# One-core hybrid trunk: a thirteenth weight buffer for a fourth split pair, group norm by chunks, and the last small expert block behind the last wide one

## The chip, the core and the metric

The kernel runs on one core of one Trainium2 chip. The metric is the device time of one execution in microseconds; lower is better. Times of the kernel before come from three runs and from one more execution, which was profiled.

## What is computed

Two residual layers over 256 tokens of width 1024, in fp32. From the reference, cut:

```python
# each layer: x = x + W_out[concat(RWKV-7 | MLA | gMLP)(rms_norm(x) @ W_in)]
#             x = x + FFN(rms_norm(x))   dense SwiGLU in layer 0, top 2 of 8 SwiGLU experts in layer 1
# RWKV-7 part (6 heads of 64), after the scan over the tokens:
mu = jnp.mean(y, axis=-1, keepdims=True)
var = jnp.mean(jnp.square(y - mu), axis=-1, keepdims=True)
y = (y - mu) * lax.rsqrt(var + RWKV_GN_EPS)
y = y * ln_g + ln_b
y = y + jnp.sum(rh * kh * r_k, axis=-1, keepdims=True) * vh
y = y.reshape(B_, S_, A_WIDTH) * g
```

An expert has an inner width of 3584: 42 MiB of weights for gate, up and down projections, so the eight experts are 336 MiB, read from HBM once per execution.

## The kernel before

The program is `mix(0)`, `ffn()`, `mix(1)`, `experts()`.

**Arithmetic.** Products of full precision are made from two halves of a number: `split` (L192 to L198) makes a high part `wh` of 1024 columns on ACT (L196) and the rest `wl` on DVE (L197), and `mm3` (L200 to L203) issues three matmuls. A pair `wh`, `wl` comes from the pools `h_p` and `l_p`, three of each, and the experts have one pair more of their own (`NHL = 1`, pools `hi2` and `lo2`, L1173 to L1175; `own` in `units`, L1401).

**mix.** A layer's mix runs its parts as generators in the order of a string, `ORDER` (L38, L39): `R` is one step of the RWKV part, `o` one of `wout` (L403 to L429), `M` and `G` the other two parts. The RWKV scan works in four chunks of 64 tokens (the loop that begins behind `norm`): each chunk's products go through `R1` (a copy on DVE), `SA` and the state `M` to `ysb`. `norm(t)` (L743 to L765) then takes 128 tokens, two chunks, at a time: square on ACT (L748), reduction on DVE (L750), a power on POOL (L214 and L209, inside a helper), four products on DVE (L755), three transposes on TensorE (L759), two operations (L762, L763) and a copy and a subtract into `yTh` and `yTl` (L764, L765). `wout` has eight weight halves; three of them, n = 5, 6 and 7, need the result of `norm`, and for these it does the first 128 tokens for all three and then the second 128. At the end `x` gets the sums (L449 to L452).

**experts.** After the router the 336 loads of 1 MiB are issued by SP in one fixed order by `eload` (L1108 to L1117), into twelve buffers in a ring, `raw2` (8) and `raw` (4). Load 12 is the first that waits for a buffer. L1114 issues loads of an expert known beforehand and those of L1116 take the expert's number from a register that is read from `order` (L1180). The experts are sorted into places p = 0 to 7 by how many tokens they may take: wide blocks (128 tokens, p = 1, 2, 3, seven blocks each, 21 in all) use split weights; small blocks (64 tokens for p = 4, 5, 6, 32 for p = 0 and 7, 35 in all) use the weights as they come. A block is six loads, four for gate and up and two for down, and a load is two halves. In the trace, L1480 and L1496 are small blocks' gate and up, L1483 or L1498 their SiLU, L1507 to L1523 their transposes and transposed copies, L1550 their down products; L201 to L203 with `xg` are a wide block's gate and up, with `aT` its down products.

`work` and `halves` follow the same table, `TURNS` (L125): the number of small blocks after each wide one, the first two of the 35 (`LEAD`) coming before all wide ones. `fill` (L1427 on) issues splits ahead of `take`, with `AHEAD = 2` and `WINDOW = 10`. An expert's sums are scaled and added to `x` by `finish` (L1362 to L1387): a scaled copy and a subtract (L1371, L1372), matmuls (L1382, L1383) and adds (L1384); for the last expert each piece is stored as soon as it is added (L1692), eight stores.

Of the kernel before, what the change touches and what calls it, by code (L numbers as in the profile page):

```python
# [32 lines left out]
NHL = 1  # L33
# [4 lines left out]
ORDER = ("a5 R2 b c a2 R a3 M2 R X R2 y R2 M G R M G M o2 R o5",  # L38
         "a5 R2 b c a2 R a3 M2 R2 X R y R2 M G R M G M o2 R o5")  # L39
# [85 lines left out]
TURNS = [2] * 7 + [2, 1, 1, 2, 1, 2, 1] + [1, 1, 2, 1, 1, 2, 1]  # L125
# [4 lines left out]
def trunk(ctx: ExitStack, tc: tile.TileContext, x_in, pos_in, wst, moe, pp_in, rr_in, sw_in, rt_in,  # L130
# [60 lines left out]

    def split(t, a, b, hp=h_p, lp=l_p, E=None):  # L192
        n = b - a
        h = hp.tile([128, 1024], F32R, name="wh", tag="wh")
        lo = lp.tile([128, 1024], F32R, name="wl", tag="wl")
        act(h[:, 0:n], t[:, a:b], AF.Copy)  # L196
        (E or V).tensor_tensor(lo[:, 0:n], t[:, a:b], h[:, 0:n].bitcast(F32), op=ALU.subtract)  # L197
        return h, lo  # L198
# [95 lines left out]
    def mix(l):  # L294
        with ExitStack() as mctx:
# [107 lines left out]
            def wout():  # L403
# [21 lines left out]
                ws = [weights(n) for n in range(5, 8)]  # L425
                for t in range(2):
                    for n in range(5, 8):
                        part(n, t, *ws[n - 5])
                    yield  # L429
# [19 lines left out]
        for t in range(2):  # L449
            for nh in range(2):  # L450
                s_ = slice(nh * 512, nh * 512 + 512)
                V.tensor_tensor(x[:, t, s_], x[:, t, s_], acc[2 * t + nh], op=ALU.add)  # L452
# [6 lines left out]
    def rwkv(l, buf, wbuf, W, lz, z3, sg, pc, env):  # L459
# [283 lines left out]
        def norm(t):  # L743

            yTh, yTl = env["yh"], env["yl"]
            yt = ysb[:, t * 6:t * 6 + 6, :]
            sq = buf("shp", (128, 514))[:, 0:384].rearrange("p (u v) -> p u v", u=6)
            act(sq, yt, AF.Square)  # L748
            ss = small([128, 6], name="gn_ss")
            V.tensor_reduce(ss, sq, axis=AX.X, op=ALU.add)  # L750
            r = rsqrt(pre_eps(ss, 6, 1.0 / 64, GN_EPS, "gn"), 6, "gn")
            yn = buf("shp", (128, 514))[:, 0:384].rearrange("p (i h v) -> p i h v", i=3, h=2)
            for cp in range(2):
                for hv in range(2):
                    V.tensor_tensor(yn[HALF[cp], :, hv, :], yt[HALF[hv], cp * 3:cp * 3 + 3],  # L755
                                    r[HALF[hv], cp * 3:cp * 3 + 3, None].to_broadcast([64, 3, 64]), op=ALU.mult)
            ps = pb()
            for i in range(3):
                T.transpose(ps[:, i * 128:i * 128 + 128], yn[:, i].rearrange("p h v -> p (h v)"), ident)  # L759
            ts = slice(t * 128, t * 128 + 128)  # L760
            ya = ga[:, :, ts]
            V.tensor_tensor(ya, ps[:, 0:384].rearrange("p (i s) -> p i s", i=3), ya, op=ALU.mult)  # L762
            V.tensor_tensor(ya, ya, bv[:, :, ts], op=ALU.add)  # L763
            act(yTh[:, 0:3, ts], ya, AF.Copy)  # L764
            V.tensor_tensor(yTl[:, 0:3, ts], ya, yTh[:, 0:3, ts].bitcast(F32), op=ALU.subtract)  # L765

        M = None
        for c in range(4):
# [24 lines left out]
            act(ysb[:, c * 3:c * 3 + 3, :], ps, AF.Copy)  # L793
            if c == 1:
                yield
                norm(0)
                yield
        yield
        norm(1)
# [300 lines left out]
    def experts():  # L1100
# [7 lines left out]
        def eload(e, j):  # L1108
            i = cnt_loads[0]
            cnt_loads[0] += 1  # L1110
            pool = raw2_p if i % (4 + NRAW2) < NRAW2 else raw_p
# [60 lines left out]
        ap_ = ctx.enter_context(tc.tile_pool(name="moa", bufs=2, reuse_waits="tile"))  # L1172
        if NHL:  # L1173
# [119 lines left out]
        assert len(TURNS) == len(wides) and LEAD + sum(TURNS) == len(narrows)  # L1293
# [114 lines left out]
        def halves():  # L1408
# [4 lines left out]
            for n in range(len(wides) + 1):  # L1413
                if n < len(wides):
                    yield from units(*wides[n], range(4))
                if n > 0:
# [3 lines left out]
                before = narrows[m:m + TURNS[n]] if n < len(wides) else []  # L1420
# [145 lines left out]
        def work():  # L1566
# [8 lines left out]
            for n in range(len(wides) + 1):  # L1575
# [26 lines left out]
                new = narrows[m:m + TURNS[n]] if n < len(wides) else []  # L1602
# [244 lines left out]
```

## Time and profile before

| | us |
|---|---|
| median of 3 runs | 1409.38 |
| lowest, highest | 1407.07, 1413.32 |
| the profiled execution | 1410.85 |
| its span | 1409.0 |
| TensorE busy | 1330.4 (94%) |
| DVE busy | 714.6 (51%) |
| ACT busy | 628.3 (45%) |
| packets of SP's loads, share of 16 DMA engines over the span | 73.3% |

The span is the time from the first to the last instruction of the profiled execution; 1.85 us lie around it. The profiled execution is 1.47 us above the median. TensorE's mean granted clock is 0.968 of 2.4 GHz. A busy share is an average over stages: the experts' stage begins near 560 us.

### The profile page before, as it was taken

What the parts mean: (1) busy time and instruction counts of PE and PEld (TensorE: products, weight loads), DVE (VectorE), ACT (ScalarE), POOL (GpSimd) and SP (SyncE); (2) the same over time, 40 slices, a digit from 0 to 9 for tenths busy, and PEclk for the clock granted to TensorE, in tenths of its full rate; (3) what the DMA queues carried; (4) which work ended last, traced back from release to release, by engine and by line L of the source; (5) the groups of instructions that cost most, each with busy time, mean ns of one, the idle gap of its engine ahead of it and who ended that gap; (6) DMA issues with size and microseconds to landing.
All of it is one profiled execution on the core that took longest, in us unless ns stands there. A gap on an engine that the chain in (4) does not pass through costs nothing. (4 is left out here: it accounts for less than half of the span.)

```text
span 1409.0 us, 24079 instructions
## 1 busy us (share of the span) xinstructions
PE 1330.4 (94%) x9860; PEld 966.7 (69%) x9860; DVE 714.6 (51%) x1053; ACT 628.3 (45%) x986; POOL 77.3 (5%) x126
## 2 busy tenths in 40 slices
PE   7988899999999888999999999999999999999986
PEld 7977678888888777775666555755766656667653
DVE  5685455455576655453335314535544446556443
ACT  7558254444475652453324313423434345444442
POOL 2250000000115110000000000000000000000000
PEclk9999999999999998999999999999999999999997
DMA  7410244555452251899999999999999999999995
GB/s 285 179 61 2 90 149 180 181 188 188 147 195 103 65 222 60 341 384 426 425 426 425 426 395 368 427 381 426 407 426 414 416 426 427 426 420 426 426 426 213
DMA packets 60437, 422.63 MB, mean 300 GB/s; under 512 B 7200, under 2 KB 8224, under 8 KB 10400
## 3 DMA queue, kind: packets, MB, share of 16 engines
q1 hardware_dynamic: 59760, 420.03, 73.3%
q8 instruction: 79, 1.29, 0.4%
q10 hardware_dynamic: 560, 1.00, 0.2%
q14 instruction: 38, 0.31, 0.1%
HBM read 419.95 MB, written 1.05 MB: 299 GB/s over the span
## 5 line engine op out<-in xcount | busy, mean ns | idle before, releaser
L197 DVE TENSOR_TENSOR wl<-raw,wh 128x1024 fp32r<-128x1024 f32 (+1 forms) x370 | 439.4, 1219 | 176.3 <-ACT wh L196 173.2
L196 ACT ACTIVATE wh<-raw 128x1024 fp32r<-128x1024 f32 (+1 forms) x370 | 379.9, 1053 | 224.1 <-PE pb L203 113.2
L202 PE MATMUL pb<-wl,xg 128*128 128x512 f32 x336 | 141.0, 420 | 12.6 <-DVE wl L197 12.0
L1480 PE MATMUL pb<-raw,xgs 128*64 128x256 f32 x1344 | 151.0, 380 | 0.0
L201 PE MATMUL pb<-wh,xg 128*128 128x512 f32 x336 | 135.5, 406 | 7.8 <-ACT wh L196 7.8
L203 PE MATMUL pb<-wh,xg 128*128 128x512 f32 x336 | 133.6, 398 | 0.0
L1480 PEld LDWEIGHTS pb<-raw,xgs 128*64 128x64 f32 x1344 | 95.0, 137 | 54.7 <-issue 9.1
L1550 PE MATMUL pa<-raw,aT 128*32 128x256 f32 (+1 forms) x1008 | 120.7, 454 | 0.6 <-ACT aT L1523 0.6
L1496 PE MATMUL pb<-raw,xgs 128*32 128x256 f32 x1344 | 93.0, 402 | 9.5 <-DMA raw<-moe 9.4
L202 PEld LDWEIGHTS pb<-wl,xg 128*128 128x128 f32 x336 | 63.9, 190 | 40.4 <-DVE wl L197 23.1
L1483 ACT ACTIVATE a<-pb,rg 128x256 f32<-128x256 f32 x21 | 10.0, 474 | 178.2 <-PE pb L1480 178.2
L1511 DVE TENSOR_TENSOR aT<-pb,aT 128x512 fp32r<-128x512 f32 x21 | 14.5, 692 | 144.9 <-ACT aT L1510 144.8
L1550 PEld LDWEIGHTS pa<-raw,aT 128*32 128x32 f32 (+1 forms) x1008 | 42.3, 118 | 63.6 <-issue 49.0
L201 PEld LDWEIGHTS pb<-wh,xg 128*128 128x128 f32 x336 | 63.8, 190 | 29.6 <-ACT wh L196 15.3
L1496 PEld LDWEIGHTS pb<-raw,xgs 128*32 128x32 f32 x1344 | 46.1, 115 | 50.2 <-issue 14.0
L202 PE MATMUL pb<-wl,hTh 128*128 128x512 f32 (+1 forms) x192 | 73.0, 380 | 0.0
L203 PEld LDWEIGHTS pb<-wh,xg 128*128 128x128 f32 x336 | 64.2, 191 | 11.8
L203 PE MATMUL pb<-wh,hTl 128*128 128x512 f32 (+1 forms) x192 | 71.6, 376 | 0.0
L202 PE MATMUL pa<-wl,aT 128*128 128x512 f32 x168 | 69.2, 412 | 0.2 <-DVE wl L197 0.2
L201 PE MATMUL pb<-wh,hTh 128*128 128x512 f32 (+1 forms) x192 | 67.4, 377 | 0.7 <-ACT hTh L284 0.7
L203 PE MATMUL pa<-wh,aT 128*128 128x512 f32 x168 | 66.3, 394 | 0.0
L1485 DVE SCALAR_TENSOR_TENSOR a<-pb,rg,a 128x256 f32<-128x256 f32 x21 | 10.2, 484 | 99.4 <-PE pb L1480 99.4
(383 smaller groups left out, 2060.4 us busy)
## 6 DMA issues: line engine op xcount, KB each, us to landing
raw<-moe SPq DMA_DIRECT2D x336, 1024.0 KB, 11.9
raw<-wst SPq DMA_DIRECT2D x54, 1024.0 KB, 4.8
raw<-wst SPq DMA_DIRECT2D x4, 832.0 KB, 5.0
area<-sw_in SPq DMA_DIRECT2D x2, 960.0 KB, 6.7
area<-sw_in SPq DMA_DIRECT2D x2, 664.0 KB, 6.2
x<-x_in SPq DMA_DIRECT2D x2, 512.0 KB, 5.3
raw<-wst SPq DMA_DIRECT2D x2, 512.0 KB, 7.1
out_dram<-x SPq DMA_DIRECT2D x8, 128.0 KB, 2.3
```

The source lines that it names most:

```text
L196: act(h[:, 0:n], t[:, a:b], AF.Copy)
L197: (E or V).tensor_tensor(lo[:, 0:n], t[:, a:b], h[:, 0:n].bitcast(F32), op=ALU.subtract)
L201: T.matmul(o, lhsT=xh, rhs=wh, start=first, stop=False)
L202: T.matmul(o, lhsT=xh, rhs=wl, start=False, stop=False)
L203: T.matmul(o, lhsT=xl, rhs=wh, start=False, stop=last)
L1480: T.matmul(ps[HALF[hv], :], lhsT=z[:, k, :], rhs=w[:, o_:o_ + 256], start=(k == 0), stop=(k == KD - 1))
L1483: act(a, ps, AF.Silu, scale=rs[0])
L1485: V.scalar_tensor_tensor(a, ps, rs[0], a, op0=ALU.mult, op1=ALU.mult)
L1496: T.matmul(ps[QUART[g], :], lhsT=z[:, k, :], rhs=ws[g // 2 * 4 + k // 2][:, o_:o_ + 256], start=(k == 0), stop=(k == KD - 1))
L1511: V.tensor_tensor(z[:, :, 1, :], p3, z[:, :, 0, :].bitcast(F32), op=ALU.subtract)
L1550: T.matmul(acc[rows, :], lhsT=aT[:, f, :], rhs=ws[f][:, g * w:g * w + w], start=(i == 0 and f == 0), stop=(i == NB - 1 and f == 3))
```

## The change

- `NHL` is 0: the experts have three split pairs, not four. In place of the fourth pair a pool `raw3` holds a thirteenth weight buffer, and the ring of `eload` is 13 long.
- The last seven entries of `TURNS` become eight: the last small block (place 7, block 6) comes after the last wide block's down products, for which `work` and `halves` go round once more; `drain()` (which finishes the additions to `x` that are under way) comes ahead of it.
- `norm` takes one chunk: a reduction over 3 columns instead of 6, two products instead of four. A new `finish(t)` does transposes, the two operations, copy and subtract in three pieces of 128 columns.
- In `ORDER` the last steps are `o6 R o2`, not `o2 R o5`, and `wout` has one more `yield`. `norm` of the last chunk is issued behind the last split's subtract, and the additions to `x` behind the last subtract of `finish(1)`.

```diff
-NHL = 1
+NHL = 0
-ORDER = ("a5 R2 b c a2 R a3 M2 R X R2 y R2 M G R M G M o2 R o5",
-         "a5 R2 b c a2 R a3 M2 R2 X R y R2 M G R M G M o2 R o5")
+ORDER = ("a5 R2 b c a2 R a3 M2 R X R2 y R2 M G R M G M o6 R o2",
+         "a5 R2 b c a2 R a3 M2 R2 X R y R2 M G R M G M o6 R o2")
-TURNS = [2] * 7 + [2, 1, 1, 2, 1, 2, 1] + [1, 1, 2, 1, 1, 2, 1]
+TURNS = [2] * 7 + [2, 1, 1, 2, 1, 2, 1] + [1, 1, 2, 1, 1, 2, 0, 1]
...
-        (E or V).tensor_tensor(lo[:, 0:n], t[:, a:b], h[:, 0:n].bitcast(F32), op=ALU.subtract)
+        last_split[0] = (E or V).tensor_tensor(lo[:, 0:n], t[:, a:b], h[:, 0:n].bitcast(F32), op=ALU.subtract)
...
                 ws = [weights(n) for n in range(5, 8)]
+                yield
...
-        for t in range(2):
-            for nh in range(2):
-                s_ = slice(nh * 512, nh * 512 + 512)
-                V.tensor_tensor(x[:, t, s_], x[:, t, s_], acc[2 * t + nh], op=ALU.add)
+        with tc.issue_after(env["end"].ins):
+            for t in range(2):
+                for nh in range(2):
+                    s_ = slice(nh * 512, nh * 512 + 512)
+                    V.tensor_tensor(x[:, t, s_], x[:, t, s_], acc[2 * t + nh], op=ALU.add)
...
-        def norm(t):
+        yn = [buf("shp", (128, 514))[:, 0:384].rearrange("p (i h v) -> p i h v", i=3, h=2) for _ in range(2)]
+
+        def norm(c):
+
+            t, cp = divmod(c, 2)
+            yt = ysb[:, c * 3:c * 3 + 3, :]
+            sq = vf.tile([128, 3, 64], F32, name="sq", tag="R1", bufs=2)
+            act(sq, yt, AF.Square)
+            ss = small([128, 3], name="gn_ss")
+            V.tensor_reduce(ss, sq, axis=AX.X, op=ALU.add)
+            r = rsqrt(pre_eps(ss, 3, 1.0 / 64, GN_EPS, "gn"), 3, "gn")
+            for hv in range(2):
+                V.tensor_tensor(yn[t][HALF[cp], :, hv, :], yt[HALF[hv]],
+                                r[HALF[hv], :, None].to_broadcast([64, 3, 64]), op=ALU.mult)
+
+        def finish(t):
...
             for i in range(3):
+                T.transpose(ps[:, i * 128:i * 128 + 128], yn[t][:, i].rearrange("p h v -> p (h v)"), ident)
+                ya = ga[:, i, ts]
+                V.tensor_tensor(ya, ps[:, i * 128:i * 128 + 128], ya, op=ALU.mult)
+                V.tensor_tensor(ya, ya, bv[:, i, ts], op=ALU.add)
+                act(yTh[:, i, ts], ya, AF.Copy)
+                last = V.tensor_tensor(yTl[:, i, ts], ya, yTh[:, i, ts].bitcast(F32), op=ALU.subtract)
+            return last
...
             act(ysb[:, c * 3:c * 3 + 3, :], ps, AF.Copy)
+            if c % 2 == 0:
+                norm(c)
             if c == 1:
                 yield
-                norm(0)
+                norm(1)
+                finish(0)
                 yield
         yield
-        norm(1)
+        with tc.issue_after(last_split[0].ins):
+            norm(3)
+        env["end"] = finish(1)
...
-            pool = raw2_p if i % (4 + NRAW2) < NRAW2 else raw_p
+            j_ = i % (5 + NRAW2)
+            pool = raw2_p if j_ < NRAW2 else raw_p if j_ < NRAW2 + 4 else raw3_p
...
+        raw3_p = ctx.enter_context(tc.tile_pool(name="raw3", bufs=1, reuse_waits="tile"))
...
-            for n in range(len(wides) + 1):
+            for n in range(len(TURNS) + 1):
...
                 small_downs(before, nT)
-                new = narrows[m:m + TURNS[n]] if n < len(wides) else []
+                if n == len(wides):
+                    drain()
+                new = narrows[m:m + TURNS[n]] if n < len(TURNS) else []
```

A program sets the order of each engine's instructions from this code and from priorities, so the places that matter are shown as it came out. Line numbers of the changed kernel are two higher near `split` and some sixteen higher in the experts.

On SP, at the start of the experts' loads, before (L1116 are loads 12 and 13; they come behind seven reads of `order` at L1180, the last of which is shown, and one of a flag at L1612; ahead of the reads stand loads 0 to 11 of L1114):

```order
L1180 TENSOR_LOAD order
L1180 ISA x2
L1612 TENSOR_LOAD flag_i
L1612 ISA x2
L1116 ISA
L1116 DMA raw<-moe 128x2048
L1116 ISA
L1116 DMA raw<-moe 128x2048
```

and changed (L1129 are loads 0 to 11, L1131 load 12, L1196 the reads):

```order
L1129 DMA raw<-moe 128x2048 x12
L1196 TENSOR_LOAD order
L1196 ISA x2
L1131 ISA
L1131 DMA raw<-moe 128x2048
L1196 TENSOR_LOAD order
L1196 ISA x2
```

Load 12 moved from behind all the reads to right behind the first; load 13 is now the first behind them.

On ACT, from one wide block of the first expert that has them to the next, before (L196 splits, L1461 the wide block's SiLU, L1498 and L1523 the 32-token block that goes with it, L1483, L1510 and L1523 the small blocks of 64 tokens):

```order
L196 ACTIVATE wh<-raw 128x1024 x6
L1461 ACTIVATE a<-pb,rg 128x512
L196 ACTIVATE wh<-raw 128x1024 x6
L1498 ACTIVATE a<-pb,rg 64x256
L1523 ACTIVATE aT<-pb 128x2x2x64 x2
L1483 ACTIVATE a<-pb,rg 128x256 x2
L1510 ACTIVATE aT<-pb 128x4x128
L1523 ACTIVATE aT<-pb 128x2x2x32
L196 ACTIVATE wh<-raw 128x1024 x7
```

and changed (L198 splits, the others sixteen lines further down):

```order
L198 ACTIVATE wh<-raw 128x1024 x6
L1477 ACTIVATE a<-pb,rg 128x512
L198 ACTIVATE wh<-raw 128x1024 x5
L1514 ACTIVATE a<-pb,rg 64x256
L1539 ACTIVATE aT<-pb 128x2x2x64 x2
L198 ACTIVATE wh<-raw 128x1024
L1499 ACTIVATE a<-pb,rg 128x256 x2
L1526 ACTIVATE aT<-pb 128x4x128
L1539 ACTIVATE aT<-pb 128x2x2x32
```

One split, the first half of the next wide block, moved ahead of the small blocks' SiLU; on DVE its subtract moved with it.

On TensorE, at the end of the program, before (L201 to L203 are the last wide block's down products, L1550 the last small block's, L1382 and L1383 what `finish` multiplies):

```order
L201 MATMUL pa<-wh,aT 128x512 x2
L1550 MATMUL pa<-raw,aT 32x256 x8
L202 MATMUL pa<-wl,aT 128x512
L203 MATMUL pa<-wh,aT 128x512
L202 MATMUL pa<-wl,aT 128x512
L203 MATMUL pa<-wh,aT 128x512
L1550 MATMUL pa<-raw,aT 32x256 x8
L1382 MATMUL pb<-oh,pT 128x512 x4
L1383 MATMUL pb<-ol,pT 128x512 x4
L1382 MATMUL pb<-oh,pT 128x256 x2
L1383 MATMUL pb<-ol,pT 128x256 x2
```

and changed (L203 to L205, L1566, L1398 and L1399 in their place; L1512 and L1536 are the last small block's gate and up and its transposes):

```order
L203 MATMUL pa<-wh,aT 128x512 x2
L204 MATMUL pa<-wl,aT 128x512
L205 MATMUL pa<-wh,aT 128x512
L204 MATMUL pa<-wl,aT 128x512
L205 MATMUL pa<-wh,aT 128x512
L1398 MATMUL pb<-oh,pT 128x512 x4
L1399 MATMUL pb<-ol,pT 128x512 x4
L1512 MATMUL pb<-raw,xgs 32x256 x32
L1536 MATMUL pb<-cc,a 128x64 x2
L1566 MATMUL pa<-raw,aT 32x256 x16
L1398 MATMUL pb<-oh,pT 128x256 x4
L1399 MATMUL pb<-ol,pT 128x256 x4
```

The last small block moved behind the last wide block and behind what `finish` does for it.

## Rows read from the trace of the kernel before

**Rows 1.** The page: busy time of the engines, and what the DMA moved in 40 slices.

```profile
PE 1330.4 (94%) x9860; PEld 966.7 (69%) x9860; DVE 714.6 (51%) x1053; ACT 628.3 (45%) x986; POOL 77.3 (5%) x126
...
GB/s 285 179 61 2 90 149 180 181 188 188 147 195 103 65 222 60 341 384 426 425 426 425 426 395 368 427 381 426 407 426 414 416 426 427 426 420 426 426 426 213
```

**Rows 2.** Windows: each engine's busy time (instructions), granted clock, DMA share, GB/s.

```profile
860.00:880.00 20.00, 20.00 (x139) 10.64 (x141) 3.84 (x5) 3.14 (x6) 0.00 (x0) 1.00 0.87 343
...
1340.00:1360.00 20.00, 14.22 (x99) 9.31 (x100) 10.52 (x10) 10.77 (x14) 0.00 (x0) 0.91 1.01 426
```

**Rows 3.** The chain of waits, its last step through the loads: start, duration, link.

```profile
1363.31 19.78 DMA raw<-moe
```

**Rows 4.** SP's own timeline at loads 11 and 12: start, duration, instruction.

```profile
538.50 0.33 SPq L1114 DMA_DIRECT2D raw<-moe  x1
568.78 2.63 SPq L1116 DMA_DIRECT2D raw<-moe  x4
```

**Rows 5.** The page, costliest groups: busy, mean ns of one, idle before and releaser.

```profile
L197 DVE TENSOR_TENSOR wl<-raw,wh 128x1024 fp32r<-128x1024 f32 (+1 forms) x370 | 439.4, 1219 | 176.3 <-ACT wh L196 173.2
L196 ACT ACTIVATE wh<-raw 128x1024 fp32r<-128x1024 f32 (+1 forms) x370 | 379.9, 1053 | 224.1 <-PE pb L203 113.2
L202 PE MATMUL pb<-wl,xg 128*128 128x512 f32 x336 | 141.0, 420 | 12.6 <-DVE wl L197 12.0
```

**Rows 6.** Timelines of ACT and then TensorE at one wide block's start.

```profile
790.81 0.47 ACT L1483 ACTIVATE a<-pb,rg 128x256 f32<-128x256 f32 x1 [6.43 <-PE pb L1480]
...
793.76 3.90 ACT L196 ACTIVATE wh<-raw 128x1024 fp32r<-128x1024 f32 x4
798.39 1.06 ACT L196 ACTIVATE wh<-raw 128x1024 fp32r<-128x1024 f32 x1 [0.73 <-PE pb L203]
799.79 1.06 ACT L196 ACTIVATE wh<-raw 128x1024 fp32r<-128x1024 f32 x1 [0.33 <-PE pb L203]
...
795.15 0.50 PE L201 MATMUL pb<-wh,xg 128*128 128x512 f32 x1
796.93 0.50 PE L202 MATMUL pb<-wl,xg 128*128 128x512 f32 x1 [1.29 <-DVE wl L197]
```

**Rows 7.** The weight buffers in 1360 to 1400 us, and the timeline of the end.

```profile
L1116 SPq DMA_DIRECT2D raw<-moe x5: 333/333/333, 1360.9 to 1371.0; - x5
...
DMA to landing us min/median/max: 19.4/19.8/19.8
...
1392.52 1.07 PE L1550 MATMUL pa<-raw,aT 128*32 128x256 f32 x16
...
1398.22 5.31 SPq L1692 DMA_DIRECT2D out_dram<-x  x8
```

**Rows 8.** Layer 0's mix at its end: timelines of DVE, POOL, TensorE; TensorE's windows.

```profile
165.05 1.23 DVE L197 TENSOR_TENSOR wl<-raw,wh 128x1024 fp32r<-128x1024 f32 x1 [1.57 <-ACT wh L196]
...
168.14 1.28 DVE L452 TENSOR_TENSOR x<-x,pa 128x512 f32<-128x512 f32 x2 [1.40 <-PE pa L203]
...
167.12 1.33 POOL L209 TENSOR_TENSOR rq_y<-pe,cc 128x6 f32<-128x6 f32 x1
...
168.18 0.40 PE L203 MATMUL pa<-wh,hTl 128*128 128x512 f32 x1
...
173.24 0.79 PE L201 MATMUL pa<-wh,hTh 128*128 128x512 f32 x1 [1.79 <-ACT hTh L764]
...
160.00:168.00 8.00, 8.00 (x43) 1.00 0.53 201
173.00:179.00 6.00, 5.76 (x14) 0.50 0.00 0
```

**Rows 9.** Layer 1's mix at its end: timeline of TensorE.

```profile
532.79 0.45 PE L739 MATMUL pb<-SA,TrbT 64*64 64x64 f32 x8
...
540.04 1.25 PE L1142 MATMUL pa<-cc,x 128*128 128x128 f32 x8
...
542.25 0.50 PE L201 MATMUL pa<-wh,hTh 128*128 128x512 f32 x1 [0.96 <-ACT hTh L764]
```

More of the change, by code (lines that the diff above doesn't have):

```diff
@@ L190, in load @@
         return t
+    last_split = [None]
     def split(t, a, b, hp=h_p, lp=l_p, E=None):
@@ L741, in chain_mm @@
             return ps[:, 0:192].rearrange("p (u c) -> p u c", u=3)
-        def norm(t):
-            yTh, yTl = env["yh"], env["yl"]
[L746 to L756, printed above, removed]
+        yn = [buf("shp", (128, 514))[:, 0:384].rearrange("p (i h v) -> p i h v", i=3, h=2) for _ in range(2)]
@@ L757, in norm @@
+        def finish(t):
+            yTh, yTl = env["yh"], env["yl"]
+            ts = slice(t * 128, t * 128 + 128)
             ps = pb()
             for i in range(3):
[L759 to L763, printed above, removed]
@@ L764, in norm @@
-            act(yTh[:, 0:3, ts], ya, AF.Copy)
-            V.tensor_tensor(yTl[:, 0:3, ts], ya, yTh[:, 0:3, ts].bitcast(F32), op=ALU.subtract)
+                T.transpose(ps[:, i * 128:i * 128 + 128], yn[t][:, i].rearrange("p h v -> p (h v)"), ident)
[4 more added lines that the diff above has]
+                last = V.tensor_tensor(yTl[:, i, ts], ya, yTh[:, i, ts].bitcast(F32), op=ALU.subtract)
@@ L1292, in experts @@
         narrows = [(p, i) for p in NARROWS for i in range(NB)]
-        assert len(TURNS) == len(wides) and LEAD + sum(TURNS) == len(narrows)
+        assert len(TURNS) == len(wides) + 1 and LEAD + sum(TURNS) == len(narrows)
         ask(0)
@@ L1412, in halves @@
                     yield from units(*b, js)
-            for n in range(len(wides) + 1):
+            for n in range(len(TURNS) + 1):
                 if n < len(wides):
                     yield from units(*wides[n], range(4))
-                if n > 0:
+                if 0 < n <= len(wides):
                     yield from units(*wides[n - 1], (4, 5))
@@ L1419, in halves @@
                     yield from units(*b, (4, 5))
-                before = narrows[m:m + TURNS[n]] if n < len(wides) else []
+                before = narrows[m:m + TURNS[n]] if n < len(TURNS) else []
                 m += len(before)
@@ L1574, in work @@
             ask(NARROWS[1])
-            for n in range(len(wides) + 1):
+            for n in range(len(TURNS) + 1):
                 if wjob is not None:
```

## The prediction

> **What bounds the kernel now.** I read the page first, then 20 us windows, then the chain of waits and the queue of SP, and last three short timelines. The page's 40 slices say that from about 600 us on 426 GB/s come in nearly without a break [rows 1]: 1 MiB in 2.46 us. Behind that are the experts' 336 loads, all issued by SP. The windows show where the stream falls short: 343 GB/s in 860 to 880 us, while TensorE is busy for 20.00 of 20 us; but in 1340 to 1360 us the DMA is full and TensorE is busy for 14.22 us only [rows 2]. So two bounds take turns: between about 740 and 1020 us the buffers are full and TensorE decides, later the stream does. The chain agrees: before its last 26 us it runs back through DMA alone, three steps of eight loads, the last one 19.78 us [rows 3], which is 2.47 us a load. A microsecond gained anywhere before the last landing thus counts only if it makes the loads start earlier; one gained behind the last landing counts whole.
>
> **The thirteenth buffer.** Loads 0 to 11 go into twelve free buffers. Load 12 is the first that must wait for one: it goes out at 568.78 us with the next three, 30 us after load 11 at 538.50 [rows 4]. With thirteen, every load waits for the buffer of one load earlier. That is worth one place in the stream, once: **-2.4 us** [rows 3], for the buffer is refilled at the same rate afterwards. Nothing delays it: in the new order of SP load 12 stands right behind the first read of the register `order`, which it needs. Bounds: 0 and -4.9 (two places).
>
> **Three split pairs.** A half of a wide load costs ACT 1.05 us and, behind it, DVE 1.22 us [rows 5]; TensorE needs 1.40 us for its six matmuls, the distance at which pairs come free in the block shown (ACT, waiting for L203, starts at 798.39 and 799.79) [rows 6]. A pair is thus held for 1.05 + 1.22 + about 0.2 of hand-over + 1.40 = 3.9 us. Shared among three that is 1.29 us a half, below TensorE's 1.40: three just keep up, while nothing else comes between on ACT and DVE. That the pairs are scarce is in the page: ACT waits 113.2 us in all for L203, the last reader of a pair [rows 5]. For a block I take 0.
>
> **The start of a wide block.** In the block shown ACT makes four splits in a row from 793.76, so all four pairs had been free; the first began only then because it stood in line behind the SiLU and the transposed copies of the small block. TensorE has its high half at 795.15 and its low half at 796.93, with 1.29 us of idle time [rows 6]. In the new order one split stands ahead of that SiLU, on ACT and on DVE. TensorE's idle time for low halves is 12.6 us over all 336 such matmuls [rows 5]; about a third of the expert stage (280 of 850 us) is bound by TensorE, so about **-4.0 us** reach the stream there. Ends: 0 (three pairs shorten the lead as much as the order lengthens it) and -9.0 (seven blocks between 745 and 1012 us at 1.29).
>
> **The end.** The last load lands 19.4 us after its issue, at 1371.0 + 19.4 = 1390.4 us; the first store goes out at 1398.22 [rows 7]: 7.8 us, in which TensorE still does a wide load's second half, L1550 only at 1392.52, both blocks' results and the adds to x. Now the last wide block, with its sums, lies ahead of the last loads, and behind the last landing are left at most the 16 matmuls of L1550 (1.07 us), one scaled copy and one subtract over 128x256 (0.47 us each, as the SiLU over as many [rows 6]), two matmuls and one add, with hand-over about 1.2 us. That is some 3.3 us. So **-4.5 us**. The eight stores behind stay (0.66 us apart, to the end of the span 10.8 us after the first); SP issues nothing else there. Ends: -3.0, if TensorE's clock, granted at 0.91 in 1340 to 1360 us where it waits for loads [rows 2], is low there, and -5.2.
>
> **The tail of mix, layer 0.** In the old order the last split ends at 166.28 us, the run of matmuls at 168.58, and they go on at 173.24 us only: between lie the group norm over six columns, with 1.33 us on POOL, and two adds to x (0.64 us each), which stand ahead of the norm's products on DVE [rows 8]. For chunk 3 alone, ready behind the split: reduction 0.35, POOL 0.20 + 0.85 (estimated for three columns, between half and all of the 1.33), two products 0.72, one transpose 0.33, two ops of 0.26, copy 0.30, and 0.5 of hand-over: 3.8 us, so 170.1. Against it stands that all of chunk 3's products now come ahead of the run, where before they were put between its matmuls; TensorE then waits for R and SA, and R waits on DVE for chunk 2's norm: +1.5. Sum **-1.6 us**, ends +1 and -5.0. The second end is the clock: behind the wait, in 173 to 179 us, it is granted at 0.50, that is 1.2 GHz, and 14 matmuls take 6 us, while in 160 to 168 us it is 1.00, 2.4 GHz, and 43 take 8 [rows 8]. Those 14 would take 2.6 us at the full clock's pace (14 x 8 / 43), 3.4 less; of this I count none, and all of it in the second end. By "TensorE: Matmul & The Clock Gate" of the Trainium skill, section "HAM oscillation — how this bites in real kernels", idle stretches between matmuls bring the lower clock; by that rule a shorter wait may keep the higher one, and this term would be -5.0.
>
> **The tail of mix, layer 1.** Old: chunk 3's last product at 533.24 us, matmuls of the second half of the tokens resumed at 542.25, with six matmuls of the last weight and waits for it in between [rows 9]. New: the product comes after 20 matmuls of the run (533.6 to 534.05, by the same run's pace); ysb, square and reduction 1.1, POOL and products 1.9, hand-over 0.4, so the transposes come near 537.4 and the first piece of hTh 1.3 later, at 538.7: -3.5. But the eight transposes of x for the router (1.25 us) filled that wait before [rows 9] and now follow the adds to x, behind the run: **-2.3 us**. Ends 0 and -4. The ffn between the layers moves as a whole, and so does the router.
>
> Sum: 2.4 + 4.0 + 4.5 + 1.6 + 2.3 = 14.8 us. The profiled execution took 1410.85 us (span 1409.0), so 1396.1; the median of the runs, 1409.38, is 1.5 below it, so **1394.6**, say 1395.
>
> **Rivals.**
> - *Three pairs starve TensorE (slower).* If adds to x (0.64 us) and SiLU (0.47 us) [rows 6, 8] fall between the splits, a pair is held for 5.0 us, 1.67 a half, 0.27 more than TensorE needs: 12 halves make 3.2 us a wide block. Seven blocks up to 1012 us make 23 us, all of it in the stream; from 0.18 us a half on, the change loses. With no gain at the block starts: 1394.6 + 4.0 + 23 = **1422**. For it speaks the 113.2 us, against it that ACT and DVE are busy for 45% and 51% of the span only [rows 1]. 0.08.
> - *The sure part alone.* The block starts stay, the mixes give nothing: 2.4 + 3.0 = 5.4, so **1404**, which is no change (within 0.5%, 7 us, about what a measurement here can tell). For it: the dips of rows 2 are TensorE's, and a buffer does not make it faster. 0.17.
> - *The early split holds the SiLU.* Where loads are late (from 1310 us on) the split placed ahead now waits for its load, and the small block's SiLU, its products and transposed copies, some 1.6 us, come after it instead of in the wait. The stream hides that except in the last such block: +1.6, and without the gain at block starts **1400**. The splits of rows 6 that stood behind the SiLU with pairs free show that ACT keeps its order. The Trainium skill's "TensorE: Matmul & The Clock Gate", section "Architectural detail: the array is 16× 32×32, not 1× 128×128", says the same of ACT and DVE, strict first-in, first-out. 0.10.
> - *More.* Layer 0 keeps its clock (-3.4 more) and the block starts give all (-5.0 more): **1386**. 0.15.
> - The forecast: 0.50.
>
> **How the numbers follow.** The forecast's own cases lie between 1389 and 1400. Eight in ten are held from just under the lower case, 1385, to the sure part alone, 1404; left out are the starved TensorE and a little at both ends. Faster by over 0.5% means below 1402.3: the forecast, the lower case and nearly all of the third rival, 0.74. Within: the sure part and the rest, 0.18. Slower: the starved TensorE, 0.08.
>
> **What would show it.** The first store about 3 us behind the last landing; load 12 issued by some 5 us sooner after load 11, and each later load at least one place earlier; no idle time of TensorE for L199 at the starts of wide blocks, and the low windows of 820 to 1020 us filled; matmuls resumed near 171.6 us in layer 0 and some 3 us earlier in layer 1. Wrong would be: TensorE waiting for L199 in the middle of wide blocks, or the same low windows with the stream shifted by 2.4 us only.

## The result, and the profile after

| | us |
|---|---|
| before, median of 11 runs (lowest, highest) | 1411.38 (1407.07, 1413.32) |
| changed, median of 11 runs (lowest, highest) | 1417.07 (1414.76, 1426.99) |
| ratio, 95% interval | 1.0053 [1.0036, 1.0070] |
| profiled execution of the changed kernel, span | 1414.76, 1412.9 |

The kernel became slower by half a per cent where 1395 was forecast. The thirteenth buffer and the new end did about what they were to do; the new norm did more than that in layer 0 and nothing in layer 1. The loss is in the blocks of the experts between about 690 and 1023 us, in which the profile shows no idle time of TensorE that had not been there before.

The page of the changed kernel, where it answers to [rows 1, 5] (L198 and L199 are the splits, L203 to L205 a wide block's three matmuls, L1566 the small blocks' down products):

```profile
PE 1345.2 (95%) x9860; PEld 966.5 (68%) x9860; DVE 724.3 (51%) x1081; ACT 635.4 (45%) x998; POOL 79.5 (6%) x134
...
L199 DVE TENSOR_TENSOR wl<-raw,wh 128x1024 fp32r<-128x1024 f32 (+1 forms) x370 | 444.7, 1220 | 197.2 <-ACT wh L198 192.3
L198 ACT ACTIVATE wh<-raw 128x1024 fp32r<-128x1024 f32 (+1 forms) x370 | 384.0, 1054 | 252.5 <-PE pb L205 157.3
L204 PE MATMUL pb<-wl,xg 128*128 128x512 f32 x336 | 142.3, 424 | 11.7 <-DVE wl L199 10.9
...
L1566 PE MATMUL pa<-raw,aT 128*32 128x256 f32 (+1 forms) x1008 | 131.8, 456 | 1.0 <-ACT aT L1539 1.0
```

ACT waits 157.3 us for the last reader of a pair (L205), before 113.2: the pairs are scarcer. But TensorE waits for them no longer than it did (10.9 us for low halves, before 12.0). It is busy for 14.8 us more, with the same 9860 instructions: the number to explain.

The windows, for [rows 2]:

```profile
820.00:840.00 20.00, 20.00 (x131) 10.08 (x127) 0.00 (x0) 0.47 (x1) 0.00 (x0) 1.00 0.83 306
860.00:880.00 20.00, 20.00 (x122) 9.91 (x121) 7.31 (x7) 5.36 (x7) 0.00 (x0) 1.00 0.76 307
```

At the full clock (1.00) TensorE is busy throughout, but in 860 to 880 us it gets through 122 matmuls where it got through 139, and the stream falls to 307 GB/s where it had 343. (The work in the two windows is not quite the same, for the blocks begin 4 to 5 us later by then; the table of block starts below counts the same work.)

SP's timeline at loads 11 and 12, for [rows 4], and at the stores:

```profile
527.71 0.33 SPq L1129 DMA_DIRECT2D raw<-moe  x1
553.26 0.35 SPq L1131 DMA_DIRECT2D raw<-moe  x1
...
1404.09 4.26 SPq L1710 DMA_DIRECT2D out_dram<-x  x8
```

The weight buffers behind 1371 us, for [rows 7]:

```profile
L1131 SPq DMA_DIRECT2D raw<-moe x5: 332/333/333, 1371.2 to 1381.0; - x5
...
DMA to landing us min/median/max: 19.5/19.5/19.9
```

Load 12 goes out 15.5 us earlier, the last load 10.0 us later. It lands 10.5 us later, at 1400.9 us. From there to the end of the span it is 12.0 us, before 18.6.

The start of every wide block (its first matmul on TensorE, from the two traces; blocks are counted from 0) says where that turns:

| wide block | 0 | 3 | 4 | 5 | 6 | 7 | 8 | 10 | 14 |
|---|---|---|---|---|---|---|---|---|---|
| before, us | 584.3 | 697.8 | 745.9 | 795.1 | 844.8 | 893.7 | 941.6 | 1013.5 | 1160.4 |
| changed, us | 579.2 | 692.8 | 743.9 | 795.8 | 848.4 | 899.2 | 949.1 | 1023.4 | 1172.8 |
| difference | -5.1 | -5.0 | -2.0 | +0.6 | +3.6 | +5.4 | +7.5 | +10.0 | +12.4 |

5.1 us are gained by the time the wide blocks begin, and 15.1 us are lost in blocks 3 to 9, which TensorE bounds: 315.6 us became 330.7. Block 5 shows how. A piece of it on TensorE before (L1496 are gate and up products of the 32-token block that runs beside the wide one; the trace has two records for each small matmul, so x30 are 15):

```profile
802.71 1.93 PE L1496 MATMUL pb<-raw,xgs 128*32 128x256 f32 x30
804.57 0.50 PE L202 MATMUL pb<-wl,xg 128*128 128x512 f32 x1
...
806.16 0.64 PE L1496 MATMUL pb<-raw,xgs 128*32 128x256 f32 x8
806.73 0.50 PE L202 MATMUL pb<-wl,xg 128*128 128x512 f32 x1
...
820.71 0.40 PE L203 MATMUL pa<-wh,aT 128*128 128x512 f32 x1
820.95 0.40 PE L202 MATMUL pa<-wl,aT 128*128 128x512 f32 x1
821.19 0.40 PE L203 MATMUL pa<-wh,aT 128*128 128x512 f32 x1
821.52 8.51 PE L1550 MATMUL pa<-raw,aT 128*32 128x256 f32 x54
```

and changed (L1512 are those products):

```profile
802.80 0.39 PE L205 MATMUL pb<-wh,xg 128*128 128x512 f32 x1
803.03 0.40 PE L203 MATMUL pb<-wh,xg 128*128 128x512 f32 x1
803.36 1.91 PE L1512 MATMUL pb<-raw,xgs 128*32 128x256 f32 x26
805.20 0.50 PE L204 MATMUL pb<-wl,xg 128*128 128x512 f32 x1
805.54 0.39 PE L205 MATMUL pb<-wh,xg 128*128 128x512 f32 x1
...
806.79 1.05 PE L1512 MATMUL pb<-raw,xgs 128*32 128x256 f32 x10
807.77 0.50 PE L204 MATMUL pb<-wl,xg 128*128 128x512 f32 x1
...
811.30 0.64 PE L1512 MATMUL pb<-raw,xgs 128*32 128x256 f32 x8
811.87 0.50 PE L203 MATMUL pb<-wh,xg 128*128 128x512 f32 x1
...
814.63 0.62 PE L1512 MATMUL pb<-raw,xgs 128*32 128x256 f32 x2
815.18 0.66 PE L1536 MATMUL pb<-cc,a 128*128 128x128 f32 x4
```

A matmul of the 32-token block (128*32 in the lines) fills 32 of 128 columns; four of them begin within 0.02 us of each other, so four are called a group here. A piece is a row of small matmuls between others, and a cut is a place where the wide ones are left for such a piece.

The price of a cut is in the starts. From one wide matmul to the next it is 0.23 us (802.80 to 803.03), from a wide to a small one 0.33 (to 803.36), and the first step among the wide ones after that is 0.34 (805.20 to 805.54). A piece of one small matmul takes 0.55 us until the next engine step (814.63 to 815.18), one of four 0.57 (811.30), one of five 0.98 (806.79), one of fifteen 1.86 (802.71, before): 0.41 to 0.43 for each group begun, however few of the four there are, and 0.14 on top. So a cut costs 0.10 + 0.11 + 0.14 = 0.35 us, and 0.41 more where it leaves a group unfilled; all of it counts as busy time. In the order of TensorE, which was there to be read ahead of the run, the 32 gate and up matmuls of this block stand in pieces of 15, 4, 5, 1 and 7 before, and of 13, 5, 4, 4, 5 and 1 now; the 16 down matmuls were 2, 3 and 11, and are 5, 3, 3, 1 and 4. Over the whole program 88 such pieces became 121, and 694 begun groups (of four, or of two for 64 tokens) 709.

In blocks 3 to 9 TensorE goes from wide to small matmuls 44 times, before 22, and begins 12 groups more: 22 x 0.35 + 12 x 0.41 = 12.6 of the 15.1 us lost there. (From wide matmuls to transposes and other matmuls of 128 columns it goes 35 times, before 34.)

### The profile page after: what moved, and what is told of

The parts are those of the page before. It is cut to its first block, busy times and chain, and to the rows that moved or that the text cites. A ratio compares the mean times of both kernels' runs of the same rounds, so it can differ in the third digit from the quotient of the medians.

```text
span 1412.9 us, 24147 instructions
## 1 busy us (share of the span) xinstructions
PE 1345.2 (95%) x9860; PEld 966.5 (68%) x9860; DVE 724.3 (51%) x1081; ACT 635.4 (45%) x998; POOL 79.5 (6%) x134
## 3 DMA queue, kind: packets, MB, share of 16 engines
q8 instruction: 79, 1.29, 0.4%
## 4 chain that ended last, share of the span: by engine, by line
PE 83%; DVE 6%; ACT 3%; DMA 3%; POOL 2%; issue 2%; SPq 0%; DVEq 0%; ACTq 0%; POOLq 0%
PE pb L1496 10%; PE pa L1566 9%; PE pb L204 9%; PE pb L205 8%; PE pb L203 8%; PE pa L204 6%; PE pa L203 6%; PE pb L1512 6%; PE pa L205 6%; DVE wl L199 3%; DMA raw<-moe 3%; PE pb L1268 1%; PE pa L373 1%; PE pa L374 1%; PE pa L375 1%
## 5 line engine op out<-in xcount | busy, mean ns | idle before, releaser
L199 DVE TENSOR_TENSOR wl<-raw,wh 128x1024 fp32r<-128x1024 f32 (+1 forms) x370 | 444.7, 1220 | 197.2 <-ACT wh L198 192.3
L198 ACT ACTIVATE wh<-raw 128x1024 fp32r<-128x1024 f32 (+1 forms) x370 | 384.0, 1054 | 252.5 <-PE pb L205 157.3
L204 PE MATMUL pb<-wl,xg 128*128 128x512 f32 x336 | 142.3, 424 | 11.7 <-DVE wl L199 10.9
L1496 PE MATMUL pb<-raw,xgs 128*64 128x256 f32 x1344 | 152.5, 381 | 0.0
L203 PE MATMUL pb<-wh,xg 128*128 128x512 f32 x336 | 136.9, 410 | 5.1 <-ACT wh L198 5.1
L205 PE MATMUL pb<-wh,xg 128*128 128x512 f32 x336 | 134.1, 399 | 0.0
L1496 PEld LDWEIGHTS pb<-raw,xgs 128*64 128x64 f32 x1344 | 97.4, 137 | 52.6 <-issue 8.2
L1566 PE MATMUL pa<-raw,aT 128*32 128x256 f32 (+1 forms) x1008 | 131.8, 456 | 1.0 <-ACT aT L1539 1.0
L1512 PE MATMUL pb<-raw,xgs 128*32 128x256 f32 x1344 | 94.6, 399 | 3.9 <-DMA raw<-moe 3.7
L1566 PEld LDWEIGHTS pa<-raw,aT 128*32 128x32 f32 (+1 forms) x1008 | 42.9, 118 | 67.7 <-issue 55.2
L1527 DVE TENSOR_TENSOR aT<-pb,aT 128x512 fp32r<-128x512 f32 x21 | 14.5, 692 | 140.9 <-ACT aT L1526 140.9
L203 PEld LDWEIGHTS pb<-wh,xg 128*128 128x128 f32 x336 | 64.1, 191 | 28.8 <-ACT wh L198 12.1
L1512 PEld LDWEIGHTS pb<-raw,xgs 128*32 128x32 f32 x1344 | 45.5, 114 | 45.1 <-issue 15.5
L205 PEld LDWEIGHTS pb<-wh,xg 128*128 128x128 f32 x336 | 64.5, 192 | 11.4
L205 PE MATMUL pb<-wh,hTl 128*128 128x512 f32 (+1 forms) x192 | 71.7, 377 | 0.2 <-DVE hTl L287 0.2
L203 PE MATMUL pb<-wh,hTh 128*128 128x512 f32 (+1 forms) x192 | 67.5, 378 | 0.1
L205 PE MATMUL pa<-wh,aT 128*128 128x512 f32 x168 | 66.5, 396 | 0.0
```

The costliest lines, as they stand in the source:

```text
L199: last_split[0] = (E or V).tensor_tensor(lo[:, 0:n], t[:, a:b], h[:, 0:n].bitcast(F32), op=ALU.subtract)
L203: T.matmul(o, lhsT=xh, rhs=wh, start=first, stop=False)
L204: T.matmul(o, lhsT=xh, rhs=wl, start=False, stop=False)
L205: T.matmul(o, lhsT=xl, rhs=wh, start=False, stop=last)
L1496: T.matmul(ps[HALF[hv], :], lhsT=z[:, k, :], rhs=w[:, o_:o_ + 256], start=(k == 0), stop=(k == KD - 1))
L1512: T.matmul(ps[QUART[g], :], lhsT=z[:, k, :], rhs=ws[g // 2 * 4 + k // 2][:, o_:o_ + 256], start=(k == 0), stop=(k == KD - 1))
```

## The experiments

Two theories stood against each other. *Cuts*: with three pairs the program that orders the instructions puts small matmuls between the wide halves more often (presumably because it expects a half later), and each cut costs TensorE time. *Starved*: three pairs make TensorE wait for halves (the prediction's rival at 1422), and the cuts are only its sign. Three more runs take the change's other parts alone. The table has the time with its ratio to the kernel before on the same chip, and for blocks 3 to 9 of the profiled execution their duration, the passages of TensorE from wide to small matmuls, and the groups begun beyond the least that these matmuls need (these from the order).

| kernel | us | ratio, 95% interval | blocks 3 to 9, us | passages | groups |
|---|---|---|---|---|---|
| before | 1410.7 to 1411.8 | | 315.6 | 22 | 7 |
| changed | 1417.07 | 1.0053 [1.0036, 1.0070] | 330.7 | 44 | 19 |
| e1 three pairs | 1430.60 | 1.0141 [1.0113, 1.0168] | 329.0 | 45 | 18 |
| e3 three pairs, 13 buffers | 1427.67 | 1.0122 [1.0098, 1.0146] | 331.0 | 47 | 20 |
| e2 the rest of the change | 1405.51 | 0.9960 [0.9943, 0.9977] | 316.5 | 19 | 8 |
| e7 norm alone | 1409.01 | 0.9986 [0.9961, 1.0011] | 316.4 | 19 | 8 |
| e8 last block alone | 1405.14 | 0.9960 [0.9936, 0.9984] | 315.7 | 22 | 7 |
| e4 changed, first join | 1410.48 | 0.9999 [0.9979, 1.0019] | 321.2 | 23 | 6 |
| e5 changed, both joins | 1396.34 | 0.9882 [0.9850, 0.9914] | 311.4 | 11 | 0 |
| e6 four pairs, both joins | 1399.63 | 0.9908 [0.9879, 0.9937] | 310.7 | 9 | 0 |
| e9 before, first join | 1407.90 | 0.9974 [0.9951, 0.9996] | 308.9 | 10 | 0 |
| e10 four pairs, cut on purpose | 1417.48 | 1.0045 [1.0022, 1.0068] | 327.4 | 50 | 5 |

By the prices above, the counts make 12.6 of the 13.4 us that e1 is longer in these blocks than the kernel before, and 14.1 of the 15.4 of e3; e9 would be 7.1 shorter and is 6.7, e5 and e6 6.7 and 7.4 shorter and are 4.2 and 4.9. They are good to some 3 us; e4 fits worse (below).

**e1, e2, e3: which part loses.** e1 is the kernel before with `NHL = 0` and nothing else; e3 is that with the thirteenth buffer; e2 is the changed kernel with the fourth pair back and twelve buffers.

```diff
-NHL = 1
+NHL = 0
```

> Edit to the kernel before: NHL = 0 alone, so three split pairs and still twelve buffers. Theory A (three pairs alone cost it: with one pair less the program's order puts the small blocks' matmuls into more pieces between the wide halves, 118 runs of them against 88, and each piece costs TensorE a few tenths of a microsecond though no wait shows): slower by 10 to 15 us, about 1422, with wide blocks 3 to 9 longer by 2 to 3 us each and no more idle time of TensorE for L197 than before. Theory B (the fourth pair is not needed; the loss is the new order of blocks or the norm): within 3 us of the kernel before. Theory C (TensorE really waits for splits): slower, with idle time before L201 or L202 grown by some 10 us.

> The change without its exchange of pair for buffer: four pairs, twelve buffers, and the rest as changed (norm by chunks, the orders of mix, last small block last). Theory A: wide blocks as long as before, and the gains of the mixes (5 us at the first wide block) and of the end (6.6 us) reach the end: 1398 to 1401. Theory B: as slow as the changed kernel, 1415 or more, since the new order of blocks or the norm does the harm. Theory C: as A.

> The kernel before with the exchange alone: three pairs and thirteen buffers. Theory A: as the run with three pairs alone, less at most one load's place, 2.4 us: 1419 to 1422. Theory B: 1409, a load's place gained and nothing lost. If the thirteenth buffer is worth more than one place where TensorE is late, this run is faster than the one with three pairs alone by 5 us or more.

The fourth pair's absence alone costs 19.9 us (1430.60 against 1410.70); norm and last block together gain 5.2 (e2). The part that loses is as *cuts* has it, but the sizes were missed: e1 and e3 are 6 to 9 us slower than expected, e2 4.5. In e1's profiled execution the span is 16.3 us longer, 13.4 of it in blocks 3 to 9 and 3.0 in the three blocks ahead of them; its six times lie at 1427 to 1428 and at 1433 us. The thirteenth buffer gives 2.9 in the median (e3 against e1), one place in the stream, with intervals that overlap; in the two profiled executions the last landing is 3.0 earlier (1404.3 against 1407.3 us). In e1 the page has TensorE's wait for a low half at what it was before [rows 5], as *cuts* has it and *starved* has not:

```profile
L202 PE MATMUL pb<-wl,xg 128*128 128x512 f32 x336 | 142.6, 424 | 12.6 <-DVE wl L197 12.1
```

**e4, e5, e6, e9: fewer cuts.** The first join holds the 32-token block's products back until the wide block's last matmul has been issued; the second does it with the down products of the other small blocks. Nothing is computed otherwise.

```diff
-        T.matmul(o, lhsT=xl, rhs=wh, start=False, stop=last)
+        last_mm[0] = T.matmul(o, lhsT=xl, rhs=wh, start=False, stop=last)
...
-                    wjob = (wp, wi, a_, quarter_up(st[1], ws) if len(st) > 1 else None)
+                    with tc.issue_after(last_mm[0].ins):
+                        aq_ = quarter_up(st[1], ws) if len(st) > 1 else None
+                    wjob = (wp, wi, a_, aq_)
...
-                        small_down(accs[p, QUARTER], QUARTER, i, aqT, ws)
+                        with tc.issue_after(last_mm[0].ins):
+                            small_down(accs[p, QUARTER], QUARTER, i, aqT, ws)
...
-                small_downs(before, nT)
+                with tc.issue_after(last_mm[0].ins) if n else ExitStack():
+                    small_downs(before, nT)
```

The last of these places is the second join. e4 is the changed kernel with the first, e5 with both; e6 is e2 (four pairs, twelve buffers) with both; e9 is the kernel before with the first alone. (The expectation of e9 says both; what ran had the first, and the 69 pieces it speaks of are that kernel's. Its and e10's "third to the ninth" are blocks 3 to 9.)

> The changed kernel, with the matmuls of a wide block's 32-token companion issued behind the wide block's last matmul (gate and up, and down likewise), so that they stand together: 87 runs of small matmuls where the changed kernel has 121. Pairs, buffers and all else as changed. Theory A (the pieces cost the time): wide blocks 3 to 9 shorter by 2 to 3 us, 1402 to 1407. Theory C (splits come too late with three pairs, and the small matmuls only filled the waits): TensorE now idles for L199 inside the blocks, and the time is the changed kernel's or longer, 1417 or more.

> The changed kernel, joined further: besides the 32-token companion's matmuls, the small blocks' down products too are issued behind the wide block's last down product; 56 runs of small matmuls, where the changed kernel has 121 and the first joining 87. Three pairs, thirteen buffers. If pieces cost what the first joining says (6.6 us for 34 pieces and 19 part-filled groups fewer): 1403 to 1406. If what is left there is due to the pairs (splits late), no gain: 1410.

> The rest of the change with four pairs and twelve buffers, joined in both ways: 55 runs of small matmuls against 86 without. Pieces: 3 to 6 us below the same without joining (1405.5), so 1400 to 1403; blocks 5 and 6 shorter by 2 us or more. If four pairs leave no cost of pieces: 1405. Against the joined kernel with three pairs and thirteen buffers it shows what the exchange is worth without pieces: a place in the stream (2.4 us) for the thirteenth buffer, if three pairs suffice.

> The kernel before with nothing but both joins: the 32-token block's gate and up products in one piece behind the wide block's last gate and up matmul, and all small blocks' down products in one piece behind its last down matmul. Four split pairs, twelve buffers, the old norm, the old end. Pieces of small matmuls in the order of TensorE: 69, before 88; in the third to the ninth wide block 19 instead of 31. Theory (pieces cost TensorE time): these seven blocks, 315.6 us before, take 311, as the two kernels with all joined (311.4 and 310.7 us with 18 pieces); about 5 us of it reach the end, so 1406, ratio 0.996 to 0.998. Rival (the joins helped those kernels only by what they do for the last block or for three pairs): 1411, ratio 1.000, and 315.6 us.

With three pairs and 11 passages the seven blocks take 311.4 us, with four pairs and 9 passages 310.7: once the cuts are gone, the fourth pair is worth nothing that can be measured, and the thirteenth buffer and three pairs together (e5 against e6) are 3.3 us ahead, with intervals that overlap. e5 is the fastest, 20.7 us below the changed kernel and 1.2% below the one before, and 7 us below what was expected of it. It has the same three pairs, ACT still waits longer for their last reader than before (135.2 us, before 113.2), and TensorE waits for low halves as long as before:

```profile
L198 ACT ACTIVATE wh<-raw 128x1024 fp32r<-128x1024 f32 (+1 forms) x370 | 384.0, 1054 | 236.7 <-PE pb L207 135.2
L206 PE MATMUL pb<-wl,xg 128*128 128x512 f32 x336 | 140.6, 418 | 12.8 <-DVE wl L199 12.0
```

e9 does the same in the kernel before: 6.7 us less in these blocks, 3.9 in the median. e4 does not fit well, and at 1410.48 it missed the 1402 to 1407 expected. It has as many passages as the kernel before, within one, and takes 5.6 us longer in these blocks, 2.5 of them because its pieces end in 64-token down products (from the last small matmul to the next wide one 0.52 us, where a 32-token piece has 0.31). The rest is open; it may be three pairs after all, up to 3 us of the 15.

**e10: more cuts with four pairs.** e6 with the 32-token block's products cut again, always after whole groups of four, and held to that order.

```diff
+                        with tc.issue_after(behind.ins) if behind is not None else ExitStack():
+                            mm3(ps, z[:, k, 0, :], z[:, k, 1, :], wh[:, s_], wl[:, s_], k == 0, k == KD - 1)
+                        if j == 1 and cut is not None and k < KD - 1:
+                            with tc.issue_after(last_mm[0].ins):
+                                behind = quarter_part(cut, ws, k)
...
+                if aqT is not None and f < 3:
+                    with tc.issue_after(last_mm[0].ins):
+                        behind = small_down(accs[p, QUARTER], QUARTER, i, aqT, {f: w}, (f,))
```

> The kernel with four pairs, twelve buffers and all joined (1399.63 us), cut again on purpose and held to that order: the 32-token block's gate and up products go four matmuls at a time (one whole group of four) behind each k of the wide block's second sum, its down products four at a time behind each f of the wide block's down products. No work is added, nothing is split otherwise, the pairs stay four. Pieces 131 instead of 55, groups 688 instead of 682; in the third to the ninth wide block 66 instead of 18. Theory (pieces cost TensorE time, four pairs or three): by the steps from start to start in the traces a whole group between two wide matmuls costs 0.30 + 0.31 - 0.25 - 0.11 = 0.25 us more than in a run of its like, so these blocks take 310.7 + 48 x 0.25 + 5 x 0.42 = 325 us, and the time is some 15 to 22 us more, 1415 to 1422, though no pair is missing. Rival (the loss is three pairs that come too late, and pieces are only its sign): with four pairs nothing is lost, 311 us and 1400, within 4.

This decides it. With four pairs and, but for a few instructions of ACT and DVE, nothing changed except the places of the small matmuls, the seven blocks take 16.7 us more (327.4 against 310.7) and the kernel 17.9 (1417.48 against 1399.63). By the prices above it would be 41 passages x 0.35 + 5 x 0.41 = 16.4. TensorE at one such place, a cut after a whole group and the next:

```profile
811.40 0.40 PE L207 MATMUL pb<-wh,xg 128*128 128x512 f32 x1
811.73 0.64 PE L1464 MATMUL pb<-raw,xgs 128*32 128x256 f32 x8
812.30 0.51 PE L205 MATMUL pb<-wh,xg 128*128 128x512 f32 x1
812.64 0.39 PE L206 MATMUL pb<-wl,xg 128*128 128x512 f32 x1
812.88 0.40 PE L207 MATMUL pb<-wh,xg 128*128 128x512 f32 x1
813.20 0.64 PE L1464 MATMUL pb<-raw,xgs 128*32 128x256 f32 x8
```

and its page:

```profile
L206 PE MATMUL pb<-wl,xg 128*128 128x512 f32 x336 | 139.0, 414 | 12.1 <-DVE wl L199 11.3
```

0.33 into the small matmuls, 0.57 for the four, 0.34 to the second wide one, and no wait named; over the whole run TensorE waits for low halves as long as ever.

**e7, e8: the other parts alone.** e7 is the kernel before with the new `norm`, `finish(t)` and `ORDER`; e8 is the kernel before with the new `TURNS` and the `drain()` that belongs to it.

> The kernel before with the norm by chunks and the orders of mix alone (four pairs, twelve buffers, blocks in the old order). If the gain at the first wide block in the changed kernel's trace (5 us) is the norm's and reaches the end: 1405 to 1407. If TensorE's stage of the experts swallows it: 1410.

> The kernel before with the last small block behind the last wide one alone. The time from the last landing to the end of the span was 18.6 us before and is 12.0 with the change: if that is this edit's and the landings stay, 1404 to 1406. If the loads' new order makes the last ones later, 1408 or more.

Norm by chunks gives 2.6 us in the median, which its interval can't tell from nothing; the last block's new place 6.5. In e8 the weight buffers had their last loads at

```profile
L1116 SPq DMA_DIRECT2D raw<-moe x5: 332/333/333, 1362.0 to 1371.8; - x5
```

and SP its stores at

```profile
1394.32 5.36 SPq L1694 DMA_DIRECT2D out_dram<-x  x8
```

so the stream is as late as before and the first store comes 3.1 us behind the last landing (1391.2 us), where it was 7.8 before.

One by one the parts make +19.9 - 2.9 - 2.6 - 6.5 = +7.9 us, measured +5.7. But e2, which has norm and last block together, gained 5.2 and not 9.1; with it the sum is +11.8. The intervals of e2, e7 and e8 (2.4 to 3.5 us each way) leave room for both, so such sums are good to some 6 us here.

## Why the prediction was wrong, step by step

**Three split pairs: this step failed.** "Three just keep up", so "For a block I take 0". That three keep up is right, within the 3 us that e4 leaves open: e5 against e6 shows it, and TensorE's waits did not grow. The step failed because it priced only how long a pair is held. `NHL` also goes into the order of TensorE, which a program writes: 88 pieces became 118 with that one number changed (e1), and each cut costs. The order of the changed kernel was at hand and showed it; it was read on ACT, on SP and at the ends of TensorE only, not in the blocks that the prediction itself had called bound by TensorE. 0 was put in place of +19.9.

**The rival on the slower side** named the right part and the right blocks, at 1422 not far off, but not the mechanism: the waits that it needs are not there, and four pairs lose as much when they are cut (e10). A 0.08 for it was low also because the cost was bounded from one mechanism alone.

**The thirteenth buffer**, -2.4: measured -2.9, and 3.0 at the last landing. Right, as far as two overlapping intervals can say.

**The start of a wide block**, -4.0: nothing at the block shown, and 1.1 us of waits for low halves over the whole run (10.9, before 12.0). The changed kernel at the same block, for [rows 6], TensorE's timeline

```profile
795.79 0.50 PE L203 MATMUL pb<-wh,xg 128*128 128x512 f32 x1
797.59 0.50 PE L204 MATMUL pb<-wl,xg 128*128 128x512 f32 x1 [1.29 <-DVE wl L199]
```

and ACT's:

```profile
794.41 2.95 ACT L198 ACTIVATE wh<-raw 128x1024 fp32r<-128x1024 f32 x3
```

The wait is 1.29 us as before. The order was misread: ACT's "x6, x5, and one behind the SiLU" holds twelve splits, which are the wide block's own twelve, so the one that changed sides is its last, which went behind the 32-token block's SiLU, and not the next block's first. The rival of the early split rests on the same misreading. Three splits now come in a row instead of four, since there are three pairs.

**The end**, -4.5 with ends -3.0 and -5.2: from the last landing to the end of the span 18.6 became 12.0 in the changed kernel (-6.6) and 13.8 in e8 (-4.8). The first store comes 3.2 us behind the landing, for which the sum had 3.3. What was taken to stay did not in this execution: the eight stores were issued in 4.26 us instead of 5.31, and the first is followed by 8.8 us instead of 10.8 (5.36 and 10.7 in e8, so the new end alone does not do it). In the other profiled executions with the new end 12.6 to 14.5 us lie behind the last landing, and 17.4 in e4 (the first store 5.1 behind the landing, the end 12.3 behind that).

**The tail of mix, layer 0**, -1.6 with -5.0 as the far end: the last matmul of `wout` starts at 173.0 us instead of 180.0, -7.0: 4.3 of it where the matmuls go on (168.94 us instead of 173.24), and 2.7 behind that, at a higher clock. TensorE's timeline, for [rows 8]:

```profile
166.57 0.40 PE L205 MATMUL pa<-wh,hTl 128*128 128x512 f32 x1
...
168.86 0.33 PE L768 MATMUL pb<-cc,shp 128*128 128x128 f32 x1 [0.39 <-DVE zv L770]
168.94 0.48 PE L203 MATMUL pa<-wh,hTh 128*128 128x512 f32 x1
```

and the windows:

```profile
168.00:174.00 6.00, 5.15 (x23) 3.86 (x24) 5.27 (x14) 3.58 (x6) 0.00 (x0) 1.00 0.20 83
173.00:179.00 6.00, 5.36 (x29) 3.70 (x28) 5.81 (x10) 4.39 (x10) 0.00 (x0) 1.00 0.46 165
```

The matmuls go on at 168.94, 2.4 us behind the last one before the wait and 1.2 before the 170.1 that the sum had, and the granted clock stays at 1.00 where it had been 0.50. So the second end came true, wait and clock, and the term was taken at less than a quarter of what came. In the windows of 173 to 179 us the five profiled kernels with the old norm have 0.50 to 0.59, the seven with the new one 1.00. The rule of the Trainium skill's "TensorE: Matmul & The Clock Gate", section "HAM oscillation — how this bites in real kernels", agrees with the trace: with the shorter wait the lower clock of 173 to 179 us (0.50 before, 1.00 now) does not come.

**The tail of mix, layer 1**, -2.3: nothing at the first wide block. The run of `wout` begins at 507.8 us instead of 513.6, so 5.9 us come in from layer 0. TensorE goes on at 533.43 us instead of 542.25 [rows 9]: 8.8, of which 2.9 are layer 1's own, near the 3.5 that the sum had. But here the new tail brings the lower clock:

```profile
533.43 0.78 PE L203 MATMUL pa<-wh,hTh 128*128 128x512 f32 x1
534.00 0.63 PE L204 MATMUL pa<-wl,hTh 128*128 128x512 f32 x1
```

It is granted at 0.50 from 533.4 to 536.5 us, behind 3.4 us in which TensorE was busy for 0.94. In the old tail the last weight's matmuls and the router's transposes stood in the wait (busy for 3.49 of 6 us, 536 to 542), and behind it the clock stayed at 1.00. So the last 18 matmuls of `wout` take 5.5 us from the first start to the last instead of 4.1. (They take 5.5 to 6.6 in six of the seven profiled kernels with the new tail, 4.0 in e5, and 4.1 in all five with the old one. That the old one kept its clock by the work in the wait was not tested.) The last of them starts 7.4 us earlier, at 538.9, and with the router's transposes now behind it, 5.1 are left at the first wide block, 0.8 less than came in (0.8 and 1.2 less in e7 and e2). Both mixes together were forecast at 3.9; layer 0 was sized too small and layer 1 too large. How much of it reaches the experts differs from one profiled execution to another (last section).

Sum by measured parts in place of -14.8: -2.9 for the buffer, 0 for the block starts, -6.5 for the end, -2.6 for both mixes (which its interval can't tell from nothing), and +19.9 where 0 stood: the +7.9 above.

## What to carry to other kernels

A change of a pool's size is also a change of the order, where a program writes the order. Count, in the stage that an engine bounds, how often that engine changes between kinds of work before and after; a bound engine that is "busy for 20.00 of 20 us" can still be slowed by it, and then no wait tells. Matmuls that fill only a part of TensorE's columns belong in one piece, in multiples of what runs side by side.

## What the runs showed that was not expected

- A begun group of small matmuls costs TensorE 0.41 to 0.43 us whether one or four of them are in it (pieces of 1, 4, 5 and 15 in 0.55, 0.57, 0.98 and 1.86 us), and a passage from wide to small matmuls and back some 0.35 us, as busy time. The Trainium skill's "TensorEngine Tiling (Array Packing)", section "Key Properties", says that changing the tiling mode (here from 128 columns to 32 or 64 and back) drains TensorE. The steps of 0.33 and 0.34 us in place of 0.23 agree; the page gives no price, and none was put into the sum.
- The new tail of mix keeps the clock at 1.00 in layer 0 and loses it in layer 1 (0.50 behind the wait), where the old one had small work in the wait. Such work may be worth its place; no run moves it alone.
- What the new norm gains in layer 0 can be lost again at the granted clock before the experts begin. The changed kernel and e2 have the same mix, and both end layer 0's `wout` near 173 us (173.0 and 173.2), but in the profiled execution of e2 the first wide block begins at 584.0 us, not at 579.2. The window 500 to 520 us, of the changed kernel:

```profile
500.00:520.00 20.00, 19.22 (x200) 16.02 (x199) 10.84 (x30) 7.90 (x18) 1.80 (x4) 1.00 0.72 283
```

and of e2:

```profile
500.00:520.00 20.00, 20.00 (x175) 17.17 (x175) 7.52 (x24) 6.07 (x15) 0.74 (x2) 0.66 0.58 211
```

The clock is granted at 1.00 (2.4 GHz) in one; 0.66 in the other is a mean of stretches at 2.4 and 1.2 GHz. e4 and e7 go with the first (blocks begin at 578.6 and 578.7), e5, e6 and e10 with the second (585.7, 583.5, 581.5), though e5 is the fastest of all. Why the clock falls in some and not in others is open. It may be part of why the runs of one kernel lie 6 to 15 us apart.
